# Splitting the first load of a weighted-sum kernel and moving its weights to another DMA queue

## The chip, the cores and the metric

The kernel runs on one core of a Trainium2 chip. A core has compute engines with instruction queues of their own; this kernel uses VectorE (DVE in the profile) and ScalarE (ACT) for arithmetic, and SyncE (SP) and ScalarE to issue DMAs. Sixteen DMA engines move the data between HBM and the on-chip memory (SBUF, 128 partitions). The DMAs that SyncE issues form one queue (q1 in the profile), those that ScalarE issues another (q10); both run on the same sixteen engines. Every DMA of this kernel spreads its 128 partitions over the sixteen engines, 8 rows to each, and a row that is contiguous on both sides is one packet.

The metric is the device time of one execution in microseconds, as the median of several runs. Less is better.

## The reference

```python
batch, seq, hidden, n_experts, k = 16, 1024, 512, 8, 2
# expert_outputs: (batch, seq, k, hidden) float32
# combine_weights: (batch, seq, k) float32

def reference(expert_outputs, combine_weights):
    weights = combine_weights[..., np.newaxis]
    return np.sum(expert_outputs * weights, axis=2).astype(np.float32)
```

For each of 16384 tokens, two rows of 512 numbers are scaled by two weights and added. Read are 67 MB of rows and 128 KB of weights, written are 34 MB.

## The kernel before

Tokens are spread over the 128 partitions, 128 tokens to each. The first 120 tokens of each partition (`main`) lie one after the other in HBM, 4 KB a token, and make ten tiles of J = 12 tokens; the last 8 tokens of each partition (`LAST`) come from the end of the arrays and make an eleventh tile. The helper `rows` (line 34) gives for a first token and a count the HBM access of either part. A load of a full tile is 6 MB, in 128 rows of 48 KB; the last is 4 MB. A store is half of that.

All weights stay in one tile `wt` (line 52), 128 x 256 numbers. Two DMAs fill it (lines 54 to 57): SyncE's queue brings the weights of the first 120 tokens (120 KB, rows of 960 B), ScalarE's those of the last 8 (8 KB, rows of 64 B). They are the first DMA of each queue. After them ScalarE loads its activation table through a dummy instruction (line 60).

The loop of line 62 goes over the eleven tiles. The tile `et` comes from a pool of four buffers, so the loads of the first four tiles wait for nothing, and the load of a later tile waits until the store of the tile four before it has landed. All loads are issued by SyncE (line 67), in order. The tiles fall into three kinds:

- Tiles 0 to 8: VectorE multiplies the whole tile by its weights in one instruction (line 72) and adds the two halves in another (line 73), which writes the result `ot` into the front of the same buffer. ScalarE issues the store (line 74).
- Tile 9: ScalarE scales the first rows token by token (line 80), VectorE the second rows at once (line 95), and adds (line 96). SyncE issues the store (line 97).
- Tile 10, of 8 tokens: ScalarE scales a token's first row (line 80) and VectorE multiplies the second and adds (line 84), token by token. SyncE issues the store (line 97).

The framework sets the semaphores: an instruction that reads a tile waits for the DMAs that wrote the part it reads. The order within each queue is that of the program.

Of the kernel before, what the change touches and what calls it, by code (L numbers as in the profile page):

```python
# [1 line left out]

# [4 lines left out]


@with_exitstack
def kernel(  # L10
    ctx: ExitStack,
    tc: tile.TileContext,
    expert_outputs: bass.AP,
    combine_weights: bass.AP,
    out: bass.AP,
):

    nc = tc.nc  # L20
    b, s, k, h = expert_outputs.shape
    assert k == 2
    n = b * s
    P = nc.NUM_PARTITIONS
    per = n // P
    assert per * P == n
    J, LAST = 12, 8
    main = per - LAST
    assert main % J == 0
    eo = expert_outputs.rearrange("b s k h -> (b s) (k h)")  # L30
    cw = combine_weights.rearrange("b s k -> (b s) k")
    o = out.rearrange("b s h -> (b s) h")

    def rows(x):

        a = x[0 : P * main, :].rearrange("(p t) f -> p t f", p=P)
        b = x[P * main : n, :].rearrange("(p t) f -> p t f", p=P)
        return lambda t, c: a[:, t : t + c, :] if t < main else b[:, t - main : t - main + c, :]

    eo, cw, o = rows(eo), rows(cw), rows(o)  # L40

    dt = mybir.dt.float32
    mult = mybir.AluOpType.mult
    add = mybir.AluOpType.add
    copy = mybir.ActivationFunctionType.Copy

    last = main // J

    wpool = ctx.enter_context(tc.tile_pool(name="w", bufs=1))
    ipool = ctx.enter_context(tc.tile_pool(name="in", bufs=4))  # L50

    wt = wpool.tile([P, per * k], dt)

    for eng, t, c in ((nc.sync, 0, main), (nc.scalar, main, LAST)):
        eng.dma_start(  # L55
            out=wt[:, k * t : k * (t + c)].rearrange("p (t k) -> p t k", k=k), in_=cw(t, c)
        )

    warm = wpool.tile([P, 1], dt)
    nc.scalar.activation(out=warm, in_=nc.const_aps.tensor(1.0, (P, 1), dt), func=copy)  # L60

    for g in range(last + 1):
        et = ipool.tile([P, J, k * h], dt)

        ot = et.rearrange("p j f -> p (j f)")[:, 0 : J * h].rearrange("p (j f) -> p j f", f=h)
        t0, c = g * J, J if g < last else LAST
        nc.sync.dma_start(out=et[:, 0:c], in_=eo(t0, c))  # L67
        if g < last - 1:

            wb = wt[:, g * J * k : (g + 1) * J * k].unsqueeze(2).to_broadcast([P, J * k, h])  # L70
            ek = et.rearrange("p j (k h) -> p (j k) h", k=k)
            nc.vector.tensor_tensor(out=ek, in0=ek, in1=wb, op=mult)  # L72
            nc.vector.tensor_tensor(out=ot, in0=et[:, :, 0:h], in1=et[:, :, h : 2 * h], op=add)  # L73
            nc.scalar.dma_start(out=o(t0, c), in_=ot)
            continue


        for i in range(c):
            t = t0 + i
            nc.scalar.activation(  # L80
                out=et[:, i, 0:h], in_=et[:, i, 0:h], func=copy, scale=wt[:, 2 * t : 2 * t + 1]
            )
            if g == last:
                nc.vector.scalar_tensor_tensor(  # L84
                    out=ot[:, i, :],
                    in0=et[:, i, h : 2 * h],
                    scalar=wt[:, 2 * t + 1 : 2 * t + 2],
                    in1=et[:, i, 0:h],
                    op0=mult,
                    op1=add,  # L90
                )
        if g < last:
            w1 = wt.rearrange("p (t k) -> p t k", k=k)[:, t0 : t0 + c, 1:2]
            x1 = et[:, :, h : 2 * h]
            nc.vector.tensor_tensor(out=x1, in0=x1, in1=w1.to_broadcast([P, c, h]), op=mult)  # L95
            nc.vector.tensor_tensor(out=ot, in0=et[:, :, 0:h], in1=x1, op=add)  # L96
        nc.sync.dma_start(out=o(t0, c), in_=ot[:, 0:c])


# [1 line left out]
_INS = ['expert_outputs', 'combine_weights']  # L101
_OUTS = [((16, 1024, 512), 'float32')]


# [23 lines left out]
```

## Time and profile before

| what | value |
|---|---|
| median of 4 runs | 240.72 us (240.26, 240.68, 240.77, 241.05) |
| the profiled execution's own time | 240.26 us |
| its span | 238.5 us |
| multiply, line 72, 128x12288 | 9 times, 12.955 us each |
| add, line 73, 128x6144 | 9 times, 6.558 us each |
| VectorE idle before line 72, for loads | 27.1 us, of it 18.4 before the first |
| load of a 6 MB tile, issue to landing | 31.9 us (median of 10); the first 17.2 |
| store of a full tile from ScalarE's queue, issue to landing | 32.5 us (median of 9) |
| weights, issue to landing | 2.1 us (main part, SyncE), 2.3 us (last part, ScalarE) |

The span is the time between the first and the last instruction in the profile of one execution. The time of that execution is somewhat longer than the span, since it takes in what lies around it. The duration of a DMA runs from its issue to its landing and holds the time in which it stands behind others in its queue. In the chain of waits "SPq L55" is the issue of line 55 by SyncE's queue, and "DMA et<-in_expert_outputs_dram" the time until a load has landed. In the slices each figure stands for a fortieth of the span.

### The profile page before, as it was taken

How to read it: one execution, taken by the hardware profiler on the slowest of the kernel's cores; microseconds unless marked ns; L12 is line 12 of the kernel's file. 1: busy time of each engine (PE TensorE's matmuls, PEld its weight loads, DVE VectorE, ACT ScalarE, POOL GpSimd, SP SyncE). 2: the span in 40 equal slices, each digit the busy share in tenths (PEclk: the TensorE clock that was granted, in tenths of full speed). 3: DMA queues.
4: the chain of work that ended last, by engine and by line, in shares of the span. 5: the costliest groups of instructions: out<-in, count | busy, mean ns of one | idle time of the engine just before them, and what ended most of it. 6: DMA issues, size and time to landing. Idle time of an engine off the chain costs nothing.

```text
span 238.5 us, 153 instructions
## 1 busy us (share of the span) xinstructions
DVE 194.0 (81%) x28; ACT 14.0 (6%) x22; POOL 0.2 (0%) x4
## 2 busy tenths in 40 slices
DVE  0009999999999999999699969979996999687630
ACT  2000000000000000000000000000000000660700
POOL 0000000000000000000000000000000000000000
DMA  8999999999999999999999999799999999999995
GB/s 286 396 511 412 396 437 482 392 420 437 392 408 453 453 408 458 400 515 404 462 396 404 441 416 511 342 458 425 499 396 462 396 404 458 419 437 437 429 429 228
DMA packets 3456, 100.80 MB, mean 423 GB/s; under 512 B 512, under 2 KB 640, under 8 KB 640
## 3 DMA queue, kind: packets, MB, share of 16 engines
q1 hardware_dynamic: 2016, 72.48, 70.9%
q10 hardware_dynamic: 1440, 28.32, 27.6%
HBM read 67.24 MB, written 33.55 MB: 423 GB/s over the span
## 4 chain that ended last, share of the span: by engine, by line
DMA 60%; DVE 33%; ACT 2%; DVEq 0%; ACTq 0%; issue 0%; SPq 0%
DMA et<-in_expert_outputs_dram 32%; DMA out_dram<-et 28%; DVE et L72 22%; DVE et L73 11%; ACT et L80 2%; DVE et L84 1%; DVEq L123 0%; ACTq L123 0%; SPq L55 0%; SPq L67 0%; DVEq L72 0%; ACTq L80 0%
## 5 line engine op out<-in xcount | busy, mean ns | idle before, releaser
L72 DVE TENSOR_TENSOR et<-et,wt 128x12288 f32<-128x12288 f32 x9 | 116.6, 12955 | 27.1 <-DMA et<-in_expert_outputs_dram 27.1
L73 DVE TENSOR_TENSOR et<-et 128x6144 f32<-128x6144 f32 x9 | 59.0, 6558 | 0.3
L80 ACT ACTIVATE et<-et,wt 128x512 f32<-128x512 f32 x20 | 12.5, 710 | 211.9 <-DMA et<-in_expert_outputs_dram 211.9
L84 DVE SCALAR_TENSOR_TENSOR et<-et,wt 128x512 f32<-128x512 f32 x8 | 5.6, 749 | 3.9 <-ACT et L80 3.7
L95 DVE TENSOR_TENSOR et<-et,wt 128x6144 f32<-128x6144 f32 x1 | 6.6, 6557 | 2.2 <-DMA et<-in_expert_outputs_dram 2.2
L96 DVE TENSOR_TENSOR et<-et 128x6144 f32<-128x6144 f32 x1 | 6.6, 6559 | 0.9 <-ACT et L80 0.9
L60 ACT ACT_TABLE_LOAD x1 | 1.3, 1283 | 1.2 <-PEq L112 1.2
L60 ACT ACTIVATE warm<-const-float32-1.0 128x1 f32<-128x1 f32 x1 | 0.2, 202 | 0.0
L112 POOL MEMSET const-bfloat16-1.0<- 128x1 bf16 x1 | 0.1, 101 | 0.0
L112 POOL MEMSET const-uint8-127<- 128x1 uint8 x1 | 0.1, 101 | 0.0
L112 POOL MEMSET const-float32-0.0<- 128x1 f32 x1 | 0.1, 98 | 0.2 <-issue 0.2
L112 POOL MEMSET const-float32-1.0<- 128x1 f32 x1 | 0.1, 98 | 0.0
## 6 DMA issues: line engine op xcount, KB each, us to landing
et<-in_expert_outputs_dram SPq DMA_DIRECT2D x10, 6144.0 KB, 31.9
out_dram<-et ACTq DMA_DIRECT2D x9, 3072.0 KB, 32.5
et<-in_expert_outputs_dram SPq DMA_DIRECT2D x1, 4096.0 KB, 27.1
out_dram<-et SPq DMA_DIRECT2D x1, 3072.0 KB, 13.8
out_dram<-et SPq DMA_DIRECT2D x1, 2048.0 KB, 9.1
wt<-in_combine_weights_dram SPq DMA_DIRECT2D x1, 120.0 KB, 2.1
wt<-in_combine_weights_dram ACTq DMA_DIRECT2D x1, 8.0 KB, 2.3
```

Of the source, the lines that this page charges most:

```text
L60: nc.scalar.activation(out=warm, in_=nc.const_aps.tensor(1.0, (P, 1), dt), func=copy)
L72: nc.vector.tensor_tensor(out=ek, in0=ek, in1=wb, op=mult)
L73: nc.vector.tensor_tensor(out=ot, in0=et[:, :, 0:h], in1=et[:, :, h : 2 * h], op=add)
L80: nc.scalar.activation(out=et[:, i, 0:h], in_=et[:, i, 0:h], func=copy, scale=wt[:, 2 * t : 2 * t + 1])
L84: nc.vector.scalar_tensor_tensor(out=ot[:, i, :], in0=et[:, i, h : 2 * h], scalar=wt[:, 2 * t + 1 : 2 * t + 2], in1=et[:, i, 0:h], op0=mul ...
L95: nc.vector.tensor_tensor(out=x1, in0=x1, in1=w1.to_broadcast([P, c, h]), op=mult)
L96: nc.vector.tensor_tensor(out=ot, in0=et[:, :, 0:h], in1=x1, op=add)
L112: nc = _bacc.Bacc("TRN2", target_bir_lowering=False, num_devices=1)
```

## The change

The two loads of the weights are both issued by ScalarE, the main part first. SyncE begins with the first tile, and this tile is loaded in two DMAs: token 0 of each partition alone (128 rows of 4 KB, 0.5 MB) and tokens 1 to 11 (128 rows of 44 KB). All other tiles are loaded as before, and the arithmetic and the stores are the same.

```diff
-    for eng, t, c in ((nc.sync, 0, main), (nc.scalar, main, LAST)):
-        eng.dma_start(
+    for t, c in ((0, main), (main, LAST)):
+        nc.scalar.dma_start(
             out=wt[:, k * t : k * (t + c)].rearrange("p (t k) -> p t k", k=k), in_=cw(t, c)
         )
...
         t0, c = g * J, J if g < last else LAST
-        nc.sync.dma_start(out=et[:, 0:c], in_=eo(t0, c))
+        for a, m in ((0, 1), (1, c - 1)) if g == 0 else ((0, c),):
+            nc.sync.dma_start(out=et[:, a : a + m], in_=eo(t0 + a, m))
```

## The prediction

> **What bounds the kernel now.** I read the page's slices and its account of the DMA queues first, because this kernel does two passes of simple arithmetic over 67 MB and must be limited either by the arithmetic engine or by the transfers.
>
> ```profile
> span 238.5 us, 153 instructions
> ...
> DVE 194.0 (81%) x28; ACT 14.0 (6%) x22; POOL 0.2 (0%) x4
> ...
> DMA  8999999999999999999999999799999999999995
> ...
> DMA packets 3456, 100.80 MB, mean 423 GB/s; under 512 B 512, under 2 KB 640, under 8 KB 640
> ```
>
> The DMA row has a 9 in nearly every slice; VectorE (DVE) is busy for 81% and waits for loads. How fast the transfers go when nothing disturbs them is in the busy time by stretches, whose last two columns are the DMA share and GB/s, and how the two queues share the engines is in the DMA account of the stretch from 60 to 230 us:
>
> ```profile
> 5.00:15.00 10.00, 0.00 (x0) 0.00 (x0) 0.00 (x0) 1.00 1.00 433
> ```
>
> ```profile
> DMA packets 2384, 73.43 MB, mean 432 GB/s; under 512 B 272, under 2 KB 272, under 8 KB 272
> ## 3 DMA queue, kind: packets, MB, share of 16 engines
> q1 hardware_dynamic: 1200, 47.87, 65.1%
> q10 hardware_dynamic: 1184, 25.56, 34.9%
> ```
>
> So the 16 DMA engines are full at 433 GB/s with loads alone and at 432 with loads (q1, SyncE's queue) and stores (q10, ScalarE's) mixed: 100.80 MB at 433 GB/s is 232.8 us of a span of 238.5. The other 5.7 us lie at the two ends and in a few hitches. From the packet records: the first packet starts at 1.73 us, the last ends at 237.31, and 1.2 us of closing semaphores follow. Between, no engine has a gap of over 60 ns; each only has slow packets. The first 48 KB row of a load takes 0.36 to 1.13 us longer than the 1.815 us that later rows take (mean 0.77), and the rows that meet the first store at 39 to 45 us lose some 0.3 to 0.7 us on each engine. One engine loses 1.6 us from 39.7 to 49.1 us and is the last at the end: fifteen engines finish between 235.9 and 236.2 us, that one at 237.31.
>
> The chain that ended last must be read with this in mind. It begins so:
>
> ```profile
> 0.67 0.07 issue
> 0.73 0.38 SPq L55
> 1.11 0.05 issue
> 1.16 17.17 DMA et<-in_expert_outputs_dram
> ...
> 18.43 12.97 DVE et L72
> ```
>
> Later it runs through VectorE three tiles long (18.4 to 76.9 us) and then through a store. It follows releases, though, and in that stretch the DMA engines are full as well. The end is set by when the stream of packets begins, how much work each engine has in it, and which engine lost most. Of the chain, only the 0.43 us of line 55 ahead of the first load (0.38 of issue, 0.05 between) touches the start of that stream.
>
> **The change, part by part.**
>
> *SyncE's weight issue goes.* The first load is now issued at 0.73 instead of 1.16 us: **-0.43 us** for the start of the load stream, and for each of the loads queued behind it (the second to fourth are issued back to back by 3.1 us). The weights' first packet came 1.0 us after its issue (0.73 to 1.73), the load's 1.08 us after its own (1.16 to 2.24), so the lag is the same and the whole 0.43 shifts.
>
> *One DMA more on SyncE's queue.* The second part of the tile is issued where the first load was before (0.38 + 0.05 later, so again 1.16), and later issues keep their places. The 1-token part is 0.52 MB, 8 rows of 4 KB on each engine. Packet times of the trace are 611 ns for 16 KB, 912 for 24, 1213 for 32 and 1815 for 48 KB: a line of 10 ns plus 27.2 bytes a ns. An estimate for a 4 KB row is then 161 ns, for a 44 KB row 1666. Eight rows are 1.29 us, so the 11-token part, with packets due at 2.24 us, is there before they are through (1.73 + 1.29 = 3.02) and the queue doesn't run dry. The price of the split is 8 more packets on each engine at 10 ns and one completion packet of 9 ns: **+0.09 us**. Here the Trainium skill speaks against the change: "DMA: Bandwidth & Descriptors", Bandwidth, asks for at least 1 MiB a DMA, and its section on the anatomy of a DMA (a fit for GpSimd's queue) gives each DMA a fixed 2.0 us. By that rule the split would cost up to 2.0 us, 242.7 in all. The row says otherwise: the first load landed at 18.33 us and the second, queued behind it, at 32.86; the 14.53 between are 6.29 MB at 433 GB/s, with nothing left for a fixed cost. I take the row, since the new part has others queued behind it as well.
>
> *The weights move to q10, beside the load.* They are 8 packets of 44 ns (960 B), 8 of 11 ns (64 B) and two completions of 9 ns on each engine, 0.46 us. Before, they ran from 1.73 to 2.44 us, while the load's first packets began at 2.43 on average: outside the load stream, in the time that SyncE's issue had left open anyway. Now they run inside it. If they all fit into the wait for the first row's data (0.77 us on average before), they cost 0; if an engine waits in line at that row and does them afterwards, 0.46. No row shows which; I take half, **+0.23**, and keep both ends.
>
> Do the weights come late? The same page, Queues, rings and completion order, says that an engine alternates between its queues packet by packet. The trace agrees: 1200 packets against 1184 on the two queues from 60 to 230 us. By that rule a weight packet waits for one load row each time, and beside rows of 44 KB the 8 of the main part take 8 x 1.67 = 13.3 us; beside 4 KB rows 8 x (0.161 + 0.044) = 1.6 us. In the good case they land near 3.8 us (with 0.4 from packet to landing, as the trace has it for weights and tiles). Should they only begin when the 4 KB rows are through, 3.0 + 13.3 + 0.4 = 16.8 us. The tile itself lands at about 18.3 - 0.1 - 0.1, so the first multiply (line 72) waits for the tile in both cases: cost 0, covered by 1.3 us. The small part (tokens 120 to 127) may trail the 44 KB rows by another 13.3 us; it is first read at line 80 at 222 us, and as a transfer it takes 0.09 us of an engine.
>
> *ScalarE.* A second issue in its queue puts the table load of line 60 some 0.4 us later (1.16 to about 1.6). Behind it stands the first store, which waits for line 73 until 38.0 us: cost 0. VectorE has one more semaphore to look at before line 72, some 0.02 us (it polls in 21 ns at 18.35), and no more work; DMA doesn't wait for it there, as its queue holds four tiles. POOL has nothing of this.
>
> *Sum*: -0.43 + 0.09 + 0.23 = **-0.11 us**, between -0.34 and +0.12. Of a span of 238.5 in an execution of 240.26 (1.76 lie around the span) that is 240.15; that execution was the fastest of those shown, 0.46 below their median of 240.72. The forecast is for the median: **240.6**.
>
> **The rivals.**
>
> *The cold start is covered (faster).* The 0.77 us that the first 48 KB row loses could belong to large rows that meet an idle queue. For: the 960 B packets before it took 44 ns almost from the first, a quarter of a microsecond at most, and later loads start with 1.815. Then 4 KB rows would start as easily and the 44 KB rows' data would be fetched meanwhile. Load data flowed in effect from 3.18 us (mean end of the first rows less 1.815). It would flow from 1.84 (mean first packet) + 0.46 + 0.09 = 2.39: -0.79, or **239.9**. Against: the start may be the latency of the load's far-spread rows, which a small row pays as well.
>
> *A queue that opens beside a running stream costs time (slower).* The only place where the trace shows that is the first store: ring q10 starts under 48 KB rows, each engine loses 0.3 to 0.7 us, one 1.6, and that one ends the kernel. Now q10 opens within the load's first microsecond. At the same price every engine loses 0.5 more, 241.1; if the engine that ends last loses 1.6 there, 242.2. I put it at **241.3**. It decides from a loss of 0.6 us on the last engine, which turns -0.11 into more than +0.48. Against: the 4 KB rows are short, and stores write to HBM, which weights don't; when later stores start, no packet is slow.
>
> *The weights don't get through (no gain by the issue slot).* If both parts trail 44 KB rows with the small one ahead, the main one lands at 3.0 + 26.7 + 0.4 = 30.1, and the first multiply is 12 us late. VectorE later stalls 8.7 us for loads (four times 2.06 to 2.28), which takes most of that up, and the DMA queue has loads until about 61 us; a gap of 1 to 3 us would appear there: **242**.
>
> **How the numbers follow.** No change within the bound has 0.52 as the forecast's case (240.25 to 240.95 by itself, with the four runs' own scatter), the covered start 0.23, the opened queue 0.21, the late weights 0.04. About 0.2% (0.48 us) is what a measurement of this kernel can tell from no change. Faster by more: 0.20 of the covered start and 0.07 of the forecast's case, 0.27. Slower by more: 0.16 of the opened queue, 0.03 of the late weights and 0.03 of the forecast's case, 0.22. Within: 0.51. The range goes from the covered start to the opened queue's place: 239.8 to 241.4.
>
> **What would show it.** The first load's packets should start at 1.73 us and the second tile land some 0.1 to 0.3 us earlier than 32.86. The second tile is the better gauge, because everything in the change is behind it. Weights landed by 4 us confirm the alternation; by 17 us, it began late. The first 44 KB rows tell about the covered start: 1.67 us each means the cold cost is gone, 2.4 that it only moved. The opened queue would show as slow packets before 5 us, on one engine above all. If the second tile lands earlier and the end does not follow, the engine that loses at the first store decides, and the prediction's idea of one stream that merely shifts is wrong.

## The result and the profile after

The changed kernel takes 239.19 us (median of 43 runs, 238.86 to 240.97), the kernel before, measured beside it, 240.25 (64 runs, 239.17 to 241.12). The ratio is 0.9969, with a 95% interval of 0.9959 to 0.998: about 0.3% or 0.75 us **faster**. It follows the means (239.49 against 240.23 us); the two medians lie 1.06 us apart, because the middle run of the one kernel falls into another group of times than that of the other. The forecast of 240.6, no change, was wrong, and the time lies below its range.

The times say more than one number. They fall into groups with gaps between them, which I bounded at 239.7 and 240.5 us after looking at them. All runs of both kernels, from this comparison and from those of the experiments below:

| kernel | runs | up to 239.7 | 239.7 to 240.5 | above 240.5 | mean |
|---|---|---|---|---|---|
| before | 305 | 60 (mean 239.35) | 181 (240.20) | 64 (240.85) | 240.17 |
| changed | 79 | 56 (239.10) | 8 (240.18) | 15 (240.73) | 239.52 |

The lowest group moved by 0.25 us, and the share of the middle group fell from 59% to 10%. Of the 0.65 us between the means 0.25 is the first, and 0.40 the second: the mean excess over the own lowest group is 240.17 - 239.35 = 0.82 before and 239.52 - 239.10 = 0.42 after.

The profile of the changed kernel is, by its time of 240.56 us, one of the highest group. These are lines of its page:

```profile
span 238.8 us, 154 instructions
...
DMA  8899999999999979999999999999999997999994
...
DMA packets 3601, 100.80 MB, mean 422 GB/s; under 512 B 529, under 2 KB 657, under 8 KB 785
...
wt<-in_combine_weights_dram ACTq DMA_DIRECT2D x1, 120.0 KB, 4.4
```

Its span is longer than the 238.5 of before, although the kernel is faster: one profile each tells nothing about a change of 0.3% when the times have groups 0.9 us apart. The additional packets are those of the split. The weights landed 4.4 us after their issue. Its chain begins so:

```profile
0.72 0.37 SPq L68
1.10 0.05 issue
1.15 17.26 DMA et<-in_expert_outputs_dram
...
18.53 12.97 DVE et L73
```

The first load is now the 4 KB part (line 68); the 44 KB part is issued at 1.15, where the first load stood before, and the tile lands at 18.4 us (18.3 before). The same kernel in another run (238.89 us, lowest group) has this page:

```profile
span 237.1 us, 154 instructions
...
DMA packets 3600, 100.80 MB, mean 425 GB/s; under 512 B 528, under 2 KB 656, under 8 KB 784
```

The second tile, which the prediction chose as its gauge, lands at 32.74 us here, at 32.94 in the first profile of the changed kernel and at 32.88 in a third, against 32.86 before. A landing waits for the last of the sixteen DMA engines and so tells little. On the mean of the engines the last row of that tile ends at 31.99 to 32.03 us in the three profiles and at 32.20 before: the stream of loads is 0.2 us earlier.

In the run of 238.89 us all sixteen DMA engines end between 235.6 and 235.98. In the profile of before one engine ended at 237.3, in that of the changed kernel above at 237.6, with the fifteen others at or before 236.2.

### The profile page after: what moved, and what is told of

It is laid out like the page before. It is cut to its first block, busy times and chain, and to the rows that moved or that the text cites. A ratio compares the mean times of both kernels' runs of the same rounds, so it can differ in the third digit from the quotient of the medians.

```text
span 238.8 us, 154 instructions
## 1 busy us (share of the span) xinstructions
DVE 194.0 (81%) x28; ACT 14.0 (6%) x22; POOL 0.2 (0%) x4
## 4 chain that ended last, share of the span: by engine, by line
DMA 46%; DVE 44%; issue 3%; ACT 2%; DVEq 0%; ACTq 0%; SPq 0%
DVE et L73 32%; DMA et<-in_expert_outputs_dram 30%; DMA out_dram<-et 16%; DVE et L74 11%; ACT et L81 2%; DVE et L85 1%; DVEq L124 0%; ACTq L124 0%; SPq L68 0%; DVEq L73 0%; ACTq L81 0%
```

## The experiments

### Which part of the change it is

Theory A: the stream starts a little earlier, and one engine falls behind in fewer runs. Theory B: the prediction's rival, a covered cold start. Three kernels ask which part of the change counts, and a fourth touches only the moment of the first store.

The changed kernel again, unedited:

> The changed kernel once more, for another profile and a second set of times. Theory A (one engine late): the gain has two parts. The stream of loads starts some 0.15 to 0.3 us earlier, and in fewer runs one DMA engine falls 1 to 1.6 us behind when the first store joins; most times should be near 239.1, some near 240.3 to 240.9, and a profile near 239.1 should have all sixteen engines end within 0.5 us of each other. Theory B (covered start): the load stream runs 0.8 us earlier in every run; the second tile lands by 32.1 us, and the engines' ends are spread as in the kernel before.

It gave 239.19 us (14 runs; 9 in the lowest group, 3 and 2 in the others), ratio 0.9981 (0.9963 to 0.9998). Theory B falls: the second tile landed 0.12 us earlier (its rows ended 0.2 us earlier on the mean of the engines), not 0.8.

The weights' move alone (the first tile in one DMA):

```diff
-    for eng, t, c in ((nc.sync, 0, main), (nc.scalar, main, LAST)):
-        eng.dma_start(
+    for t, c in ((0, main), (main, LAST)):
+        nc.scalar.dma_start(
...
```

> The first tile is one DMA of 48 KB rows; all weights go out in ScalarE's queue. Both theories: the weights alternate with 48 KB rows and land at 15 to 18 us. Theory A: the load stream starts 0.2 to 0.4 us earlier than before; ratio 0.998 to 0.999 if the share of late engines stays as before, 0.996 to 0.997 if the weights' place in the other queue is what makes them rarer. Theory B: the first rows are cold 48 KB rows again, so ratio 0.998 to 1.0.

Ratio 0.9971 (0.9959 to 0.9984), 239.21 us; 14, 7 and 1 of 22 runs in the three groups. That is the whole gain, without the split. The weights did come late, as the alternation of packets has it. From its DMA account, the last figure being microseconds from issue to landing, and from its timeline:

```profile
wt<-in_combine_weights_dram ACTq DMA_DIRECT2D x1, 120.0 KB, 17.7
wt<-in_combine_weights_dram ACTq DMA_DIRECT2D x1, 8.0 KB, 31.8
```

```profile
18.40 12.96 DVE L72 TENSOR_TENSOR et<-et,wt 128x12288 f32<-128x12288 f32 x1 [18.40 <-DMA wt<-in_combine_weights_dram]
```

Eight packets beside eight rows of 1.815 us are 14.5 us, and the landing at 18.38 is 0.18 later than the tile's own (18.20). The first multiply now waits for its weights, and the kernel is no slower for it.

The split alone:

```diff
-        nc.sync.dma_start(out=et[:, 0:c], in_=eo(t0, c))
+        for x, m in ((0, 1), (1, c - 1)) if g == 0 else ((0, c),):
+            nc.sync.dma_start(out=et[:, x : x + m], in_=eo(t0 + x, m))
```

> The first tile is loaded as 1 and 11 tokens; the weights stay where they were before, the main part first in SyncE's queue. Theory A: no earlier start, 0.1 us for the additional packets; ratio 1.000 if the late engines stay as frequent, 0.998 if the split makes them rarer. Theory B: the cold start is covered by the 4 KB rows, ratio 0.997 to 0.998 and the second tile lands 0.5 us or more earlier than 32.86.

Ratio 1.001 (0.9995 to 1.0025), 240.48 us; 6, 5 and 11 of 22. The second tile landed at 32.84. The split brings nothing by itself that these runs can tell.

The kernel before, with the first store delayed by a small VectorE addition:

```diff
+    idle = wpool.tile([P, 512], dt)
...
+            if g == 0:
+                nc.vector.tensor_tensor(out=idle, in0=et[:, 0, 0:512], in1=et[:, 1, 0:512], op=add)
             nc.vector.tensor_tensor(out=ot, in0=et[:, :, 0:h], in1=et[:, :, h : 2 * h], op=add)
```

> The kernel before with a VectorE addition of 512 columns (some 0.6 us) into a tile of its own between line 72 and line 73 of tile 0 alone: the first store meets the load stream 0.6 us later within the 1.8 us rhythm of the 48 KB rows; all else is the same. Theory A: the share of runs with a late engine changes (from some 5 in 6 of the kernel before), and the median moves by 0.4 us or more, down or up, although the work grows. Theory B: nothing that it speaks of is touched; ratio 0.999 to 1.001.

Ratio 0.9982 (0.9966 to 0.9997), 239.36 us; 16, 3 and 3 of 22. A kernel with more work and nothing of the change gets more than half of its gain. Its addition took 0.69 us. The moment of the first store matters.

### Where the first store meets the rows

Theory E, formed from the packet records of these profiles: the loads have the DMA engines to themselves until the first store, and each engine goes through rows of 1.815 us in a rhythm of its own, the sixteen spread over some 0.55 us. The store's rows can be taken from about 1.67 us after its issue, and an engine that begins a load row later than that takes a store row next; one that has begun earlier puts another load row first. When a single engine takes the store ahead, its next load row takes over 2.7 us instead of 1.8 (2.95 before), while the other engines' rows take about 2.3, and that engine is late to the end. The DMA account of the stretch from 40.5 to 42.6 us shows it. Before:

```profile
DMA packets 17, 0.81 MB, mean 386 GB/s; under 512 B 0, under 2 KB 0, under 8 KB 0
## 3 DMA queue, kind: packets, MB, share of 16 engines
q1 hardware_dynamic: 16, 0.79, 109.5%
q10 hardware_dynamic: 1, 0.02, 2.7%
```

and the changed kernel in its run of 238.89 us:

```profile
DMA packets 16, 0.79 MB, mean 374 GB/s; under 512 B 0, under 2 KB 0, under 8 KB 0
## 3 DMA queue, kind: packets, MB, share of 16 engines
q1 hardware_dynamic: 16, 0.79, 104.3%
```

Queue q10 carries the stores, and q1 the loads. Before, one store row starts in this stretch, at 41.61 us on one engine, and the load row behind it took 2.95 us; the fifteen others begin the store at 43.3 to 43.7. In the second profile all sixteen take a load row first. The early engine of before lost 1.60 us in slow rows and is the one that ends at 237.31; the others lost 0.34 to 0.89.

As a rule for the single engine the theory is not exact. The early engine of before had begun its load row 1.68 us after the store's issue, and another, which had begun 1.72 us after it, took a load row next. In the run with 1.5 us of delay below, engines that had begun 1.61 to 2.08 us after the issue took the store, and others at 1.49 to 1.92 a load. What decides for one engine stays open; the test is whether late runs come and go with the moment of the store.

The gauge that I use below is the last engine's row start of that round less the store's issue (38.01 before): 1.72 us in the profile of before, 1.64 in each of the first two of the changed kernel and 1.65 in the third, 1.64 with the weights' move alone.

A delay of 0.2 us, from an addition of 8 columns at the same place:

> The kernel before with a VectorE addition of 8 columns between line 72 and line 73 of tile 0, which puts the first store some 0.2 us later. Theory E (edge): each DMA engine has fixed what it does next when it begins a row; the first store's rows are there some 1.67 us after their issue, which in the kernel before falls within 0.05 us of the last engine's row start. An engine that begins its row after that takes the store's row ahead of the load's, alone of the sixteen, and ends 1 to 1.6 us late. A delay of 0.2 us takes all engines across: the share of runs above 239.7 us falls from about 3 in 4 to 1 in 3 or less, ratio 0.997 to 0.9985. Theory W (the early start, or the weights' queue, makes late engines rare and the store's moment is nothing to it): share and time stay, ratio 0.999 to 1.001.

Ratio 0.9975 (0.996 to 0.9991), 239.45 us. Of 22 runs 15 were in the lowest group, 1 in the middle and 6 in the highest, against 9, 49 and 17 of the 75 runs of before beside it. The middle group is all but gone; theory W has no account of it. The highest group stayed.

Delays of 1.5 us in the kernel before (1236 columns), and of 0.7 and 1.7 in the changed one (512 and 1424):

> The same with 1236 columns: the first store some 1.5 us later, so that its rows arrive in the midst of the engines' row starts, which are spread over 0.55 us of a rhythm of 1.815. Theory E: several engines take the store first and others the load; late engines in most runs, nearly none near 239.3, ratio 1.000 to 1.004. Theory W: as the kernel before, or 0.2 us more at most, with its share of low times.

> The changed kernel with an addition of 512 columns at the same place, 0.73 us later. Theory E: it keeps its 0.25 us of earlier stream and lies farther from the edge; share of late runs a quarter or less, median 239.1, ratio 0.995 to 0.9972. Theory W: as the changed kernel.

> The changed kernel with 1424 columns: 1.7 us later, one rhythm less 0.1, so that the first store's rows arrive just inside the last engines' row starts of the next round. Theory E: late engines come back, three runs in four or more above 239.7, median 239.9 to 240.6, ratio 0.998 to 1.001. Theory W: as the changed kernel, ratio 0.996 to 0.9975.

They gave 0.9982 (0.9973 to 0.9991), 0.998 (0.9971 to 0.999) and 0.9992 (0.9982 to 1.0003). The first two ratios are misses; the third lies where theory E had it. The times show why: the groups are blurred, the lowest runs are at 239.53, 239.43 and 239.53, and only 2, 0 and 0 runs lie above 240.5. In the profile with 1.5 us nine engines took the store at 43.3 to 43.8 and seven a row later, and the engines lost twice: 1.04 us of slow rows per engine from 4.5 us on, about 1.0 with 0.7 us of delay (eleven and five), against 0.45 to 0.65 in the other seven profiles of the lowest group. With 1.7 us of delay one engine alone took a store row ahead, at 43.4 us, and ended at 237.0 while the others ended by 236.5. So in these profiles a single early engine was late by itself, and a divided field cost everyone half a microsecond, which theory E had not foreseen. Later isn't simply better.

### Is it the 0.08 us of the changed kernel?

Theory F: not the store's moment, but the early start or the weights' queue makes late engines rare there. Three kernels: the weights of the last 8 tokens taken from beside the first tile and issued by SyncE behind the fourth load; the changed kernel 0.2 us later; the split alone 0.2 us later.

```diff
+    weights(nc.scalar, 0, main)
...
+        if g == 3:
+            weights(nc.sync, main, LAST)
```

> The changed kernel, with the weights of the last 8 tokens issued by SyncE behind the fourth load, so that nothing of ScalarE's queue runs beside the rows of 44 KB. From the last engine's row start to the issue of the first store (the margin: 1.72 us in the kernel before, 1.64 in the changed one, late above some 1.67), theory E: the tile's landing is no longer held up by 0.06 us, the margin grows to about 1.70, late runs come back, above half over 239.7 us; lowest times stay near 238.9; ratio 0.9975 to 1.0. Theory F (the load stream's earlier start, or the weights out of SyncE's way, is what makes late runs rare): as the changed kernel, a quarter to a third above 239.7, ratio 0.996 to 0.9975.

> The changed kernel with an addition of 8 columns between the two instructions of tile 0: margin 1.64 less 0.17, 1.47. Theory E: late runs a third or fewer, lowest times 239.0 or less and no second loss as with 0.73 us; ratio 0.9955 to 0.997, at best the fastest of all. Theory F: as the changed kernel.

> The split alone (weights as before, where 16 of 22 runs were above 239.7) with the same addition of 8 columns. Theory E: the share above 239.7 falls to a third or so, ratio 0.997 to 0.9985. Theory F: stays near three quarters, ratio 1.000 to 1.002.

The first took 240.7 us, ratio 1.004 (1.0016 to 1.0063). Its late runs came back, but as 13 of 19 above 240.5, four of them at 242.5 to 242.7, which no other kernel had; the gauge in its profile (a run of 239.2) was 1.63, not 1.70. Theory E doesn't explain this, and what else this edit disturbs is open. The second had 7, 1 and 6 of 14, ratio 1.0 (0.9977 to 1.0023), a miss: the middle group was small already, and the highest was larger in these 14 runs. The third had 9, 1 and 4 of 14, median 239.37, ratio 0.9993 (0.9971 to 1.0015): the share fell as expected, the ratio was missed by the highest group.

The strongest test goes the other way, and moves the first store of the changed kernel *earlier* by a little. Token 0, which has landed long before, is multiplied ahead, and most of what that saves is put back as an idle addition:

```diff
+    idle = wpool.tile([P, 768], dt)
...
-            nc.vector.tensor_tensor(out=ek, in0=ek, in1=wb, op=mult)
+            for x, y in ((0, k), (k, J * k)) if g == 0 else ((0, J * k),):
+                nc.vector.tensor_tensor(out=ek[:, x:y], in0=ek[:, x:y], in1=wb[:, x:y], op=mult)
+            if g == 0:
+                ef = et.rearrange("p j f -> p (j f)")
+                nc.vector.tensor_tensor(out=idle, in0=ef[:, 0:768], in1=ef[:, 2048:2816], op=add)
```

> The changed kernel, with line 72 of tile 0 in two instructions (token 0 as soon as it has landed, tokens 1 to 11 after the second part) and an addition of 768 columns between multiply and add of tile 0: the first store moves by 1.11 us forward and 1.00 back, about 0.1 us earlier than in the changed kernel. Theory E: margin 1.74, the group one engine 1.0 us late (239.7 to 240.5) returns in half of the runs, ratio 0.998 to 1.0. Theory F (early start or queue): as the changed kernel, one run in seven in that group, ratio 0.996 to 0.998.

240.06 us, ratio 0.9999 (0.9982 to 1.0016): no gain is left. Of 14 runs 2 were in the lowest group, 11 in the middle, 1 in the highest. From its timeline and from its DMA account of 40.5 to 42.6 us:

```profile
5.05 1.23 DVE L75 TENSOR_TENSOR et<-et,wt 128x1024 f32<-128x1024 f32 x1 [5.05 <-DMA wt<-in_combine_weights_dram]
18.34 11.89 DVE L75 TENSOR_TENSOR et<-et,wt 128x11264 f32<-128x11264 f32 x1 [12.07 <-DMA et<-in_expert_outputs_dram]
30.27 0.96 DVE L78 TENSOR_TENSOR idle<-et 128x768 f32<-128x768 f32 x1
...
37.85 0.35 ACTq L80 DMA_DIRECT2D out_dram<-et  x1
```

```profile
DMA packets 18, 0.84 MB, mean 398 GB/s; under 512 B 0, under 2 KB 0, under 8 KB 0
## 3 DMA queue, kind: packets, MB, share of 16 engines
q1 hardware_dynamic: 16, 0.79, 112.7%
q10 hardware_dynamic: 2, 0.05, 5.4%
```

The store is issued 19.54 us after the tile's landing instead of 19.71, the gauge is 1.79, and two engines take a store row ahead. Here is the busy time by stretches near the end, the last two columns being DMA share and GB/s, for the kernel before, the changed kernel at 238.89 us, and this one:

```profile
236.05:236.60 0.55, 0.00 (x0) 0.00 (x0) 0.00 (x0) 1.00 0.07 30
236.60:238.40 1.80, 0.00 (x0) 0.00 (x0) 0.00 (x0) 1.00 0.02 9
```

```profile
236.05:236.60 0.55, 0.00 (x0) 0.00 (x0) 0.00 (x0) 1.00 0.00 0
236.60:238.40 1.80, 0.00 (x0) 0.00 (x0) 0.00 (x0) 1.00 0.00 0
```

```profile
236.05:236.60 0.55, 0.00 (x0) 0.00 (x0) 0.00 (x0) 1.00 0.14 60
236.60:238.40 1.80, 0.00 (x0) 0.00 (x0) 0.00 (x0) 1.00 0.00 0
```

In the profile without a late engine nothing moves any longer. In the other two a few hundredths of the DMA engines' share, one or two engines of sixteen, is all that the microsecond consists of. The two late engines here ended at 237.0 and 237.1 us.

Three more went with it: the same without the idle addition, so that the first store goes out 1.1 us earlier; the weights' move without the split and with 0.2 us of delay; and the changed kernel once more.

> The same without the addition: VectorE multiplies token 0 while it waits for the other eleven and the first store goes out 1.1 us earlier. Theory E: 1.1 earlier is 0.7 later within the rhythm of 1.815, so it should look like the changed kernel 0.73 us later (no run at 239.1, none late by 1.5, median 239.7), ratio 0.997 to 0.999; the 1.1 us themselves are worth nothing. Theory F: VectorE's earlier start gives the changed kernel's time or up to 1 us less, ratio 0.992 to 0.997.

> The weights' move without the split, with the addition of 8 columns. Theory E: the group 1.0 us late (7 of 22 runs without it) shrinks to one or two, lowest times 238.9, median 239.0 to 239.2, ratio 0.9955 to 0.9975. Theory F: as the weights' move alone, 0.997 with its group between.

> The changed kernel once more, beside the others on the same chip: two runs in three below 239.5, the rest split between 240.2 and 240.8; ratio 0.996 to 0.998. Both theories.

The first: 239.36 us, ratio 0.9975 (0.9957 to 0.9993), 11, 1 and 2 of 14. The 1.1 us of VectorE's early start are worth nothing beyond the changed kernel, as expected, but the likeness to a delay of 0.7 us was a miss: fifteen engines took the store together one row earlier (41.4 to 41.7 us). In that profile (240.61 us) the sixteenth took a load row instead and was the late one, at 237.7 us. The second: **239.10 us, ratio 0.9964 (0.9951 to 0.9977)**, 20, 1 and 1 of 22, the lowest median of all; its interval overlaps that of the changed kernel, so the two can't be told apart, and this one has one DMA less. Its delay is this line:

```profile
31.55 0.17 DVE L76 TENSOR_TENSOR idle<-et 128x8 f32<-128x8 f32 x1
```

The third: 239.19 us, ratio 0.9984 (0.9968 to 1.0), 16, 0 and 6 of 22. In all three sets of the changed kernel the median was 239.19.

In order of the gauge, read from one profile of each kernel, the middle group has 3 of 22 runs at 1.00 us (before, 0.7 us later), 1 of 22, 14, 14 and 22 at 1.38 to 1.52 (the four with the addition of 8 columns), 3 of 19 at 1.63 (the small weights moved), 8 of 79 at 1.64 to 1.65 (the changed kernel) and 7 of 22 at 1.64 (the weights' move alone), 181 of 305 at 1.72 (before), 20 of 21 at 1.78 (changed, 1.7 us later) and 11 of 14 at 1.79 (the store moved earlier). In the profiles of the other four kernels the sixteen engines were not in one such round. So the group grows over the step from 1.64 to 1.72, though the gauge is not all: 8 of 79 and 7 of 22 stand at the same value. The later store alone all but empties the group in the kernel before, and the earlier store alone fills it in the changed kernel, whose early start and weights' queue stay as they are; against theory F, these two alone do not make the gain. That the changed kernel owes its smaller group to just the 0.08 us is read from the order above, since no run moves its store by so little.

## Why the prediction was wrong

**The bound was read rightly.** The sixteen DMA engines are full, the end is set by the start of the stream and by the engine that loses most. No kernel here gained by an earlier multiply.

**The early start was right in kind and too small in size.** The sum had -0.11 us, between -0.34 and +0.12; the lowest group moved by -0.25. With -0.43 and +0.09 kept, the weights would have cost 0.09 instead of the 0.23 taken; only the sum is measured, not these terms. The price of the split can't be told from nothing: the lowest group of the weights' move alone is at 239.11, with the split at 239.10. The rule of 1 MiB a DMA was rightly left aside.

**The alternation held.** The main weights landed by 5.1 us on the last engine beside 4 KB rows, where the sum had 3.8, and at 18.4 beside rows of 48 KB. The sum was short in part because the eight 4 KB rows took 1.8 to 1.9 us of an engine, not 1.29. That the multiply waits longer costs nothing in itself.

**The covered start was not it**, although its 239.9 came nearest to the gain of 0.75: its mechanism needed the second tile 0.79 us earlier, and it was 0.12 (0.2 on the mean of the engines). Yet the sign that the prediction had set down for it appeared: the first 44 KB rows took 1.67 us each. They began at 4.1 to 4.2 us on the mean of the engines. The slow start had moved into the 4 KB rows before them, in the split alone as well (1.8 us for the eight), so that sign could not tell a covered start from a moved one. The opened queue cost nothing visible when the weights opened it.

**The step that failed** is in the paragraph on ScalarE and VectorE: "VectorE has one more semaphore to look at before line 72, some 0.02 us ... DMA doesn't wait for it there, as its queue holds four tiles." That DMA doesn't wait was true, and nothing was put in the sum for the first store's moment. Relative to the engines' rows it moved by some 0.08 us. The look at the semaphores is 0.03 us longer (19.71 instead of 19.68 us from landing to store), and the first tile lands 0.43 instead of 0.35 us after the end of its last row; 0.03 goes the other way. The later landing goes with the weights' move and not with the split: it is 0.42 to 0.46 us in all eleven profiles with the main weights in ScalarE's queue, and 0.31 to 0.38 in the six without. What causes it is open. The prediction had the late engine on record, with its 1.6 us and its place at the first store, and took it for a fixed loss that the change leaves alone. It is an event that happens in most runs or in few, depending on tenths of a microsecond: a move of 0.2 us later took the middle group from 65% of the runs of before to 1 in 22, and one of about 0.15 us earlier brought it back from 10% in the changed kernel to 11 of 14. Of the 0.65 us between the means the smaller middle group is the 0.40, which the sum had at nothing.

**The range** failed with it. The four runs shown (240.26 to 241.05) were read as scatter about 240.72; against the groups now known, one is of the middle and three are of the highest. The median of before over 64 runs was 240.25, so the absolute forecast stood 0.47 us too high before the change was considered.

**What stays open:** the highest group, 1.5 us late. In the profile of the changed kernel it was one engine, last in the rhythm, that lost its time in small parts (0.72 us at 41.6, then 0.35 and 0.46 at 60 and 65), not by a store ahead of a load. In the profile of the split alone (240.7 us), of this group too, two engines did take a store ahead, at 42.2 and 42.3 us, and were late. The group had 21% of the runs before and 19% after, 11 of 22 with the split alone and 1 of 22 in each of the kernels with the weights' move alone, with and without delay; no run here tells what sets it off. Nor is it shown for each run of the middle group that a store went ahead: of the four profiles of that group three have it (before, the test that moved the store earlier, and the changed kernel with 1.7 us of delay). In the fourth, of the split alone with 0.2 us of delay (240.41 us), no store went ahead, and the latest engine had lost 1.5 us in its first load row already.

## What to carry to other kernels

Where the DMA queues are full from end to end, look at which of the sixteen engines ends last and where it lost its time; a step that nobody waits for may still decide that, by when it lets another queue begin. Before a forecast of tenths of a per cent, look for groups in the times: a change can move the share of a group without moving the groups. And a gain of this kind is fragile: a VectorE instruction of 0.2 us gave the kernel before most of it, and moving the first store of the changed kernel 0.15 us earlier took it away.

## What the runs showed that I had not expected

A single engine of sixteen that takes another queue's row out of turn was about 1 us late at the end of a run of 240, 195 us after the event, since no engine has a gap in which to catch up. When about half of the engines did so (nine and seven), none was late but they lost some 0.5 us more each. In the profile of before the first store's rows began 3.6 us after its issue on one engine and 5.3 to 5.7 us after it on the fifteen others, against 1.07 us from the issue of the first load to its first row.
